# Spreading the DMA sums of w_down over the earlier stages of a hybrid pooling / RG-LRU / ConvFFN layer

## The chip, the cores and the metric

One core of one Trainium2 chip runs the whole layer as one program. The metric is the device time of one execution in microseconds (us). TensorE (PE) multiplies, VectorE (DVE) and ScalarE (ACT) do elementwise work, GpSimd (POOL) does a little arithmetic and issues DMAs, SyncE (SP) only issues DMAs.

## The reference, cut to what matters

One layer on 1024 tokens of width 1024 (a 16 x 64 grid) with 256 context tokens, all in float32:

```python
h = rmsnorm(x, g) * (1 + sc1) + sh1
u_pool, u_lru, u_gate, g_pool, g_lru = split(h @ w_in)
y_pool = grouped(pool(u_pool) - u_pool) @ pool_w * pool_scale
y_lru  = (scan_fwd(u_lru) + scan_bwd(u_lru)) * gelu(u_gate)
m = sigmoid(g_pool) * (y_pool @ w_proj_pool) + sigmoid(g_lru) * (y_lru @ w_proj_lru)
x = x + ga1 * rmsnorm(m @ w_out, g_post_mix)
g, u = split((rmsnorm(x, g_pre) * (1 + sc2) + sh2) @ w_up)     # 2 x 3072 columns
f = (gelu(conv3x3(g) + b) * u) @ w_down                        # 3072 -> 1024
out = x + ga2 * rmsnorm(f, g_post)
```

## The kernel before, in words

Every matrix product is done in three passes: both operands are split into a high float32r part (an ACT copy) and a low rest (a DVE subtraction), L89. The program goes through these stages, one after the other in time:

- **mixing** (to about 290 us): input norm, modulation, the pooling and gelu-gate units of w_in, pooling products. Stores: sg_d (L299), gl_d (L364), yp_d (L384).
- **LRU** (to about 570 us): for each of 8 channel blocks the input unit, four gate products, the scans, one sigmoid-gate unit. Stores: sg_d (L465), yl_d (L535). The square in the recurrence (L514) is POOL's.
- **projection** (to about 800 us): the remaining gate units with their sg_d stores (L575), the reloads of yp_d and yl_d (L566, L579), the two projections, whose result is stored to m_d (L604). Then the output projection (L706) and the first norm.
- **FFN up** (about 893 to 1400 us): 24 steps f. Each step makes one 128-channel pair of the gate and up halves by a seven-product block scheme, runs the 3 x 3 convolution on DVE (L900), the gelu on ACT (L912), the product on DVE (L913), and stores it to gu_d through POOL's queue (L917). For the seven products the weights of a step (two 512 KB loads from w_up, L681 and L796) are added together and split (L797 to L804).
- **FFN down** (to the end): the same scheme with seven products over 12 pairs p; it needs sums of blocks of w_down (sd_d) as well as w_down itself. finish (L1029) makes the last norm and the residual from x1_d and stores the output rows; half h = 1 is finished after product 5, half h = 0 after product 6, which is the last.

The sums sd_d are made by DMA alone, in the buffer n2raw. For each of the 12 pairs, sum_steps (L850) gives five steps: two plain loads, three accumulating DMAs, two accumulating DMAs, one accumulating DMA, two stores to sd_d. That is 10 DMAs for each pair, all issued from POOL's queue, and each step works on what the step before it left in n2raw, so it waits until that has landed. In the kernel before, the 60 steps are issued in the FFN up stage, three behind each step f from f = 0, so that they are done at f = 19:

```python
for _ in range(3):
    g = next(steps, None)
    if g is not None:
        with tc.issue_after(chain[-1].ins):
            chain.append(next(g)[-1])
```

n2raw also holds a term of the FFN input between the end of the projection stage (L674) and the start of the FFN (L764, L768), and a copy of u at f = 21 and 22 (L905).

The order on each engine is set by the planner's priorities, which follow the order of the program unless a line raises them; issue_after puts an instruction behind a given one on the same queue. An engine's queue is worked off in order: an instruction that waits holds up all that stand behind it. The w_up loads go through SP's queue into a ring of four buffers (tag raw, three of them, and rx): a load is issued when the DVE splits that read the buffer's old contents are done, and the ACT split (L89) of what it brings stands in ACT's queue ahead of the copy fk (L810), which frees a product's PSUM for the next.

Of the kernel before, what the change touches and what calls it, by code (L numbers as in the profile page):

```python
# [8 lines left out]
F32 = mybir.dt.float32  # L9
F32R = mybir.dt.float32r  # L10
AF = mybir.ActivationFunctionType
ALU = mybir.AluOpType
# [5 lines left out]
P = 128  # L18
# [22 lines left out]
def block_kernel(ctx: ExitStack, tc: tile.TileContext, x, cx, vecs, rowv, icnt, w_mod1, w_mod, w_in, pool_w,  # L41
                 lru_w, w_pp, w_pl, w_out, w_up, w_down, out):
    nc = tc.nc
    V, A, G, T = nc.vector, nc.scalar, nc.gpsimd, nc.tensor
# [18 lines left out]
    yl_d = tc.dram_tile([KT, P, SEQ], F32, name="yl_d")  # L63
    yp_d = tc.dram_tile([KT, P, SEQ], F32, name="yp_d")
    sg_d = tc.dram_tile([KT, P, 2, SEQ], F32, name="sg_d")
    gl_d = tc.dram_tile([KT, P, SEQ], F32, name="gl_d")
    m_d = tc.dram_tile([KT, P, SEQ], F32, name="m_d")
    x1_d = tc.dram_tile([SEQ, D], F32, name="x1_d")
# [12 lines left out]
    def uid(s):  # L81
        nm[0] += 1
        return f"{s}{nm[0]}"
# [14 lines left out]
        return w  # L98

    n2raw = gpool.tile([P, 4, 512], F32, name="n2raw", tag="n2raw")  # L100
    epsc = cpool.tile([P, 1], F32, name="epsc")
    G.memset(epsc, EPS)

# [183 lines left out]
    with tc.tile_pool(name="z1", bufs=1, reuse_waits="tile") as zp:  # L287
# [5 lines left out]
        def gate_unit(which, c):  # L293
            w = wload(24 + 8 * which + c)
            ps = pp.tile([P, SEQ], F32, name=uid("pg"), tag="pu")
            mm = unit_mm(ps, w, hx_act)
            s = zp.tile([P, SEQ], F32, name=uid("sg"), tag="sg", bufs=2)
            A.activation(s, ps, AF.Tanh, scale=0.5)
            G.dma_start(sg_d[c, :, which, :], s)  # L299
            return mm  # L300

        ds, pws, invs = {}, {}, {}
# [54 lines left out]
        def ug_unit(c):  # L357
            wu = wload(16 + c)
            pu = pp.tile([P, SEQ], F32, name=uid("pu"), tag="pu")
            n_unit[0] += 1  # L360
            mm = unit_mm(pu, wu, hx_act, half_outer=n_unit[0] <= NHO)
            gl = zp.tile([P, SEQ], F32, name=uid("gl"), tag="sg", bufs=2)
            A.activation(gl, pu, AF.Gelu_apprx_tanh)
            G.dma_start(gl_d[c], gl)  # L364
            return mm

        def pool_out(g, o, after):
            pw = pws[g]
            c = 2 * g + o
            yp = zp.tile([P, SEQ], F32, name=uid("yp"), tag="yp", bufs=2)  # L370
            for h in range(2):
                hs = slice(h * 512, (h + 1) * 512)
                ps = pp.tile([P, 512], F32, name=uid("pw"), tag="py", bufs=2)
                with tc.issue_after(after.ins):
                    for k in range(2):
                        for i, (wi, ai) in enumerate(((0, 0), (0, 1), (1, 0))):
                            T.matmul(ps, pw[:, wi, o, k, :], ds[2 * g + k][:, ai, hs],
                                     start=(k == 0 and i == 0), stop=(k == 1 and i == 2))
                with tc.high_priority(offset=YPRI):
                    if h == 0:  # L380
                        A.activation(yp[:, hs], ps, AF.Copy, scale=vcol("pool_scale", c))
                    else:
                        V.tensor_scalar(yp[:, hs], ps, vcol("pool_scale", c), None, op0=ALU.mult)
            G.dma_start(yp_d[c], yp)  # L384

        ctx_t = {}

# [66 lines left out]
    with tc.tile_pool(name="z2", bufs=1, reuse_waits="tile") as zp, \  # L454
# [3 lines left out]
        def gate_unit(which, c):  # L458
            w = load_w(w_in[24 + 8 * which + c])
            ps = pp.tile([P, SEQ], F32, name=uid("pg"), tag="pu", bufs=2)  # L460
            unit_mm(ps, w, hx_act)
            s = zp.tile([P, SEQ], F32, name=uid("sg"), tag="sg", bufs=2)
            with tc.high_priority(offset=SPRI):
                A.activation(s, ps, AF.Tanh, scale=0.5)
            G.dma_start(sg_d[c, :, which, :], s)  # L465

        LC = SEQ

# [19 lines left out]
        def lru_scan(c, xp, xc, wg):  # L488
# [43 lines left out]
            y = is_[0][:, 0:SEQ]  # L532
            V.tensor_add(y, y, is_[1][:, 0:SEQ])
            V.tensor_mul(y, y, gl)
            G.dma_start(yl_d[c], y)  # L535

        gq = [(0, c) for c in range(6)] + [(1, c) for c in range(KT)]
        mods = mod_steps(zp, pp, (2, 3), 2)
# [15 lines left out]
    with tc.tile_pool(name="pj", bufs=1, reuse_waits="tile") as zp:  # L554
# [14 lines left out]
        for j, (which, c) in enumerate(gq):  # L569
            w = load_w(w_in[24 + 8 * which + c])  # L570
            ps = pbank("bbcdbb"[j])
            unit_mm(ps, w, hx_act)
            s = zp.tile([P, SEQ], F32, name=uid("sg"), tag="mq", bufs=NMQ)
            A.activation(s, ps, AF.Tanh, scale=0.5)
            G.dma_start(sg_d[c, :, which, :], s)  # L575
        hy = H("hy")
        for c in range(KT):
            st = stage()
# [17 lines left out]
        def pl_unit(c):  # L596
            mp = mps.pop(c)
            s = sg_load(1, c)
            w = load_w(w_pl[c])
            ps = pbank("b")  # L600
            unit_mm(ps, w, lambda h, k, i: hy[:, h, k, i, :])
            V.scalar_tensor_tensor(s, s, 1.0, ps, op0=ALU.add, op1=ALU.mult)
            V.tensor_add(s, s, mp)
            G.dma_start(m_d[c], s)  # L604
            return s

        n_pc = [0]
# [43 lines left out]
            bcs.append(t)  # L651
        ga1g, B2, S2 = bcs

        h2 = H("h2")
        xos = []
        LATE = 5
# [96 lines left out]
    with tc.tile_pool(name="ff", bufs=1, reuse_waits="tile") as zp:  # L753
# [93 lines left out]
                V.tensor_sub(gc[:, 0, 512:1024], v, u4)  # L847
            st[f] = (gc, u2)

        def sum_steps(p):  # L850
            n2v = n2raw.rearrange("p (g h) c -> p g h c", g=2)
            lo, up = w_down[p * P:(p + 1) * P, :], w_down[(NH + p) * P:(NH + p + 1) * P, :]
            hv = lambda a: a.rearrange("p (h c) -> p h c", h=2)
            add = lambda dst, src: G.dma_start(dst, src, accum_op=ALU.add)  # L854
            yield G.dma_start(n2v[:, 0], hv(lo)), G.dma_start(n2v[:, 1], hv(up))
            yield (add(n2v[:, 1], hv(lo)), add(n2v[:, 0, 0, :], lo[:, 512:1024]),
                   add(n2v[:, 0, 1, :], lo[:, 0:512]))
            yield add(n2v[:, 1, 0, :], lo[:, 512:1024]), add(n2v[:, 0, 0, :], up[:, 512:1024])
            yield add(n2v[:, 1, 0, :], up[:, 512:1024]),
            yield tuple(G.dma_start(sd_d[p, i], n2v[:, i].rearrange("p h c -> p (h c)")) for i in range(2))  # L860

        steps = iter([st_ for p in range(NH) for st_ in [sum_steps(p)] * 5])
        chain = []

        def tail(f):
# [97 lines left out]
        for f in range(NF):  # L963
            if f + 1 < NF:
                weights(f + 1)
            mid(f)
            if f + 1 < NF:
                head(f + 1)
            tail(f)
            if f + 1 < NF:  # L970
                post(f)
            for _ in range(3):
                g = next(steps, None)
                if g is not None:
                    with tc.issue_after(chain[-1].ins):
                        chain.append(next(g)[-1])
        pre = [down_set(0, p, gpool.tile([P, D], F32, name=uid("raw"), tag="raw", bufs=3),
                        gpool.tile([P, 2, D], F32R, name=uid("whl"), tag="whl", bufs=3)) for p in range(NPRE)]

# [30 lines left out]
    with tc.tile_pool(name="dn", bufs=1, reuse_waits="tile") as zp:  # L1010
# [3 lines left out]
        def mms(q, p, op, t):  # L1014
            dst, first = PRODS[q][:2]
            for i, (gi, wi) in enumerate(((0, 0), (0, 1), (1, 0))):
                T.matmul(bank[dst](t), op[:, gi, 512 + t * P:512 + (t + 1) * P], op[:, wi, H0],  # L1017
                         start=(first and p == 0 and i == 0), stop=(p == NH - 1 and i == 2), skip_group_check=True)
# [7 lines left out]
        s0 = zp.tile([P, 16], F32, name="s0")  # L1026
        EPRI = 150

        def finish(h, t):  # L1029
            tt = 4 * h + t  # L1030
            xr = zp.tile([P, 2, 512], F32, name=uid("xr"), tag="xr", bufs=2)
            nc.sync.dma_start(xr, x1_d[tt * P:(tt + 1) * P, :].rearrange("p (h c) -> p h c", h=2))
            ss = small.tile([P, 1], F32, name=uid("ss"), tag="ss1", bufs=3)
            if h:
                y = CB[:, :, t, :]
                with tc.high_priority(offset=EPRI):
                    A.copy(CB[:, 0, t, :], bank["X"](t))
                A.activation(jk, y, AF.Square, accum_out=ss)
                V.tensor_mul(y, y, gah)
            else:  # L1040
                y = CA[:, :, t, :]
                V.tensor_sub(CA[:, 1, t, :], bank["Y"](t), CA[:, 1, t, :])  # L1042
                A.activation(jk[:, 1, :], CA[:, 1, t, :], AF.Square, accum_out=s0[:, 4 + t:5 + t])
                V.tensor_mul(CA[:, 1, t, :], CA[:, 1, t, :], gah[:, 1, :])
                V.tensor_add(ss, s0[:, t:t + 1], s0[:, 4 + t:5 + t])
            r = rstd_of(ss, 1)
            od = out[tt * P:(tt + 1) * P, :].rearrange("p (h c) -> p h c", h=2)
            for o in (slice(0, 1), slice(1, 2)) if tt == 3 else (slice(0, 2),):
                V.scalar_tensor_tensor(xr[:, o, :], y[:, o, :], r[:, 0:1], xr[:, o, :], op0=ALU.mult, op1=ALU.add)
                nc.sync.dma_start(od[:, o, :], xr[:, o, :])  # L1050

        GRP = 6
        for q in range(7):
            last = NH - GRP if q == 6 else NH
            for p in range(last):
                op = get(q, p)
                for t in range(4):
                    mms(q, p, op, t)
            if q == 6:
                ops = [get(q, p) for p in range(last, NH)]  # L1060
            for t in range(4):
# [97 lines left out]
```

## Time and profile before

| | |
|---|---|
| runs, median (lowest to highest) | 1640.2 us (1632.53 to 1645.49), 3 runs |
| the profiled execution | 1641.79 us, span 1640.0 us |
| PE busy | 1568.3 us, 96% of the span |
| DVE busy | 1210.5 us, 74% |
| ACT busy | 687.0 us, 42% |
| POOL busy | 239.3 us, 15% |
| mean granted clock of TensorE | 0.987 of full speed |
| moved by DMA | 289.15 MB |

The span runs from the first to the last instruction of the profiled execution; the time of an execution holds about 1.8 us more. [...]

### The profile page before, as it was taken

Reading aid. Unit: us, or ns where it says so; the run is one execution under the profiler, and the core shown is the slowest. Engines: PE = TensorE matmul, PEld = TensorE weight load, DVE = VectorE, ACT = ScalarE, POOL = GpSimd, SP = SyncE. Lnnn points to the kernel's source line nnn. Section 1 sums busy time; section 2 is a strip of 40 time slices with the busy share of each in tenths; the row PEclk is TensorE's granted clock in tenths of the full one; section 3 lists DMA queues with packets and bytes.
Section 4 is the critical chain, followed back from the end, with each engine's and each line's share of the span. In section 5 each row is a group of like instructions: output and inputs, shape, how many; then the busy total and the mean of one; then the engine's idle time right before and its main releaser. Section 6 shows DMA issues by size and latency. Waiting matters only on the chain.

```text
span 1640.0 us, 18320 instructions
## 1 busy us (share of the span) xinstructions
PE 1568.3 (96%) x6976; PEld 1265.2 (77%) x6976; DVE 1210.5 (74%) x1368; ACT 687.0 (42%) x828; POOL 239.3 (15%) x328
## 2 busy tenths in 40 slices
PE   6899999999999999999999989999899999999997
PEld 4588888877778788888788768877677777888885
DVE  7777664787887654354378889998798889787567
ACT  8523322565567734122143334333333334445442
POOL 1400200111112211010110122222222220000000
PEclk9999999999999999999999999999999999999999
DMA  8335454324233266399344567777667673687555
GB/s 314 114 103 165 138 184 139 127 97 148 84 103 116 90 232 230 124 289 300 131 141 142 209 195 186 193 199 197 176 183 180 178 187 110 217 320 256 175 188 192
DMA packets 98358, 289.15 MB, mean 176 GB/s; under 512 B 10871, under 2 KB 10999, under 8 KB 97502
## 3 DMA queue, kind: packets, MB, share of 16 engines
q1 hardware_dynamic: 60926, 170.64, 31.7%
q0 software_dynamic: 37344, 117.34, 24.2%
q8 instruction: 54, 0.88, 0.2%
q14 instruction: 34, 0.28, 0.1%
HBM read 221.34 MB, written 66.60 MB: 176 GB/s over the span
## 4 chain that ended last, share of the span: by engine, by line
PE 32%; DVE 10%; DMA 6%; ACT 2%; issue 2%; SPq 0%; DVEq 0%; ACTq 0%
PE pb L740 7%; PE pb L1017 6%; PE pb L706 5%; PE pc L740 4%; DMA raw<-in_w_up_dram 4%; PE pd L1017 4%; DVE gc L900 4%; PE pd L740 3%; PE pc L1017 2%; DVE wf L89 1%; DMA out_dram<-xr 1%; ACT wf L89 1%; DVE raw L801 0%; DMA xr<-x_d 0%; DVE w L89 0%
## 5 line engine op out<-in xcount | busy, mean ns | idle before, releaser
L242 PE MATMUL pu<-hx,whl 128*128 128x512 f32 x1056 | 266.7, 392 | 1.4 <-DVE whl L89 1.4
L900 DVE SCALAR_TENSOR_TENSOR gc<-gc,vec 128x945 f32<-128x945 f32 (+1 forms) x192 | 234.2, 1220 | 4.7 <-ACT gc L886 1.8
L89 ACT CAST whl<-raw 128x1024 fp32r<-128x1024 f32 (+1 forms) x109 | 109.1, 1003 | 305.8 <-DMA raw<-in_w_up_dram 74.4
L242 PEld LDWEIGHTS pu<-hx,whl 128*128 128x128 f32 x1056 | 186.8, 188 | 39.5 <-DVE whl L89 2.0
L89 DVE TENSOR_TENSOR whl<-raw,whl 128x1024 fp32r<-128x1024 f32 (+1 forms) x109 | 128.0, 1177 | 93.7 <-ACT whl L89 93.4
L242 PE MATMUL pg<-hx,whl 128*128 128x512 f32 x480 | 117.1, 396 | 0.0
L740 PE MATMUL pb<-h,wf 128*128 128x512 f32 x384 | 96.3, 400 | 11.3 <-ACT fk L810 11.3
L242 PEld LDWEIGHTS pg<-hx,whl 128*128 128x128 f32 x480 | 89.5, 191 | 19.3
L740 PEld LDWEIGHTS pb<-h,wf 128*128 128x128 f32 x384 | 71.8, 191 | 31.5 <-ACT fk L810 16.9
L740 PE MATMUL pb<-h,whl 128*128 128x512 f32 x384 | 94.9, 393 | 0.0
L706 PE MATMUL pb<-whl,mH 128*128 128x512 f32 x384 | 89.1, 392 | 1.0 <-ACT mH L700 1.0
L242 PE MATMUL pb<-hy,whl 128*128 128x512 f32 x384 | 87.8, 389 | 0.0
L706 PEld LDWEIGHTS pb<-whl,mH 128*128 128x128 f32 x384 | 71.5, 188 | 16.6 <-ACT mH L700 1.5
L740 PEld LDWEIGHTS pb<-h,whl 128*128 128x128 f32 x384 | 71.2, 188 | 16.9 <-ACT fk L810 2.5
L242 PEld LDWEIGHTS pb<-hy,whl 128*128 128x128 f32 x384 | 72.1, 188 | 14.9
L854 POOL DMA_DIRECT2D n2raw<-in_w_down_dram x72 | 63.0, 1006 | 122.9 <-DMA n2raw<-in_w_down_dram 122.6
L740 PE MATMUL pc<-nf,wf 128*128 128x512 f32 x288 | 72.9, 402 | 6.3 <-DVE gc L875 6.2
L1017 PE MATMUL pb<-hD 128*128 128x512 f32 x306 | 78.0, 390 | 0.0
L740 PEld LDWEIGHTS pc<-nf,wf 128*128 128x128 f32 x288 | 53.6, 190 | 22.5 <-DVE gc L875 11.5
L740 PE MATMUL pc<-nf,w 128*128 128x512 f32 x288 | 70.0, 391 | 0.2 <-DVE gc L847 0.2
L498 PE MATMUL pg<-xp,whl 128*128 128x512 f32 x192 | 61.3, 416 | 7.7 <-ACT i L504 7.6
L1017 PEld LDWEIGHTS pb<-hD 128*128 128x128 f32 x306 | 57.3, 188 | 12.3 <-DVE CA L1042 0.3
(319 smaller groups left out, 2986.9 us busy)
## 6 DMA issues: line engine op xcount, KB each, us to landing
raw<-in_w_up_dram SPq DMA_DIRECT2D x41, 512.0 KB, 4.6
raw<-in_w_in_dram SPq DMA_DIRECT2D x40, 512.0 KB, 4.7
n2raw<-in_w_down_dram POOLq DMA_DIRECT2D x36, 512.0 KB, 6.0
rawm<-in_w_mod_dram SPq DMA_DIRECT2D x32, 512.0 KB, 4.1
n2raw<-in_w_down_dram POOLq DMA_DIRECT2D x60, 256.0 KB, 5.7
rw<-gu_d SPq DMA_DIRECT2D x58, 256.0 KB, 5.1
gu_d<-gc POOLq DMA_DIRECT2D x24, 512.0 KB, 3.2
sd_d<-n2raw POOLq DMA_DIRECT2D x24, 512.0 KB, 4.6
```

Of the source, the lines that this page charges most:

```text
L89: return A.copy(hi, src), V.tensor_sub(lo, src, f32(hi))
L242: mm = T.matmul(ps[:, h * 512:(h + 1) * 512], wv[:, wi, k, :], act(h, k, ai), start=st, stop=sp)
L498: T.matmul(pg[:, h * 512:(h + 1) * 512], wg[:, wi, m, :], xp[:, ai, h * 512:(h + 1) * 512], start=(i == 0), stop=(i == 2))
L706: mm = T.matmul(ps[:, h * 512:(h + 1) * 512], mh[ai][:, k, :], wo[k][:, wi, h * 512:(h + 1) * 512], start=(k == 0 and i == 0), stop=(k == ...
L740: mm = T.matmul(ps, w(wi, j), b(ai, j), start=(start and j == 0 and i == 0), stop=(j == 3 and i == 2), skip_group_check=True)
L854: add = lambda dst, src: G.dma_start(dst, src, accum_op=ALU.add)
L900: V.scalar_tensor_tensor(o, gv[:, r0 + dr:r1 + dr, c0 + dc:c1 + dc], cw(i, j), o, op0=ALU.mult, op1=ALU.add)
L1017: T.matmul(bank[dst](t), op[:, gi, 512 + t * P:512 + (t + 1) * P], op[:, wi, H0], start=(first and p == 0 and i == 0), stop=(p == NH - 1 a ...
```

## The change

45 of the 60 steps are issued earlier: sum_step puts one step behind each store of the mixing, LRU and projection stages (there are 48 such stores; the first 45 get one, which makes pairs p = 0 to 8). The other 15 are issued in the FFN up stage, one behind each step f from f = 2 to f = 16. At the end of the program, the rows of x1_d that half h = 0 needs are loaded after product 5 into the first half of N, which no one reads any more then, in place of a buffer of two that the outputs also leave from.

```diff
+    def sum_steps(p):
+        ...
+    dsteps = [st_ for p in range(NH) for st_ in [sum_steps(p)] * 5]
+    n_step = [0]
+
+    def sum_step(after, limit=45):
+        if n_step[0] >= limit:
+            return after
+        with tc.issue_after(after.ins):
+            i = next(dsteps[n_step[0]])[-1]
+        n_step[0] += 1
+        return i
...
-            G.dma_start(sg_d[c, :, which, :], s)
+            sum_step(G.dma_start(sg_d[c, :, which, :], s))
...
-            G.dma_start(yl_d[c], y)
+            sum_step(G.dma_start(yl_d[c], y))
...
-            for _ in range(3):
-                g = next(steps, None)
-                if g is not None:
-                    with tc.issue_after(chain[-1].ins):
-                        chain.append(next(g)[-1])
+            if f > 1:
+                chain.append(sum_step(chain[-1], 60))
...
+        def load_x(xr, tt):
+            nc.sync.dma_start(xr, x1_d[tt * P:(tt + 1) * P, :].rearrange("p (h c) -> p h c", h=2))
+
         def finish(h, t):
             tt = 4 * h + t
-            xr = zp.tile([P, 2, 512], F32, name=uid("xr"), tag="xr", bufs=2)
-            nc.sync.dma_start(xr, x1_d[tt * P:(tt + 1) * P, :].rearrange("p (h c) -> p h c", h=2))
+            xr = N[:, 0, 2 * t:2 * t + 2, :] if h == 0 else zp.tile([P, 2, 512], F32, name=uid("xr"), tag="xr", bufs=2)
+            if h:
+                load_x(xr, tt)
...
+            if q == 5:
+                for t in range(4):
+                    load_x(N[:, 0, 2 * t:2 * t + 2, :], t)
```

The stores of gl_d, yp_d and m_d and the other two places that store sg_d are changed in the same way.

## Rows read from the trace of the kernel before

**Rows 1.** Windows of 100 us: busy us (instructions) by engine, granted clock, DMA share, GB/s.

```profile
700.00:800.00 100.00, 99.11 (x438) 81.79 (x436) 47.16 (x48) 22.59 (x26) 10.70 (x17) 1.00 0.81 263
...
900.00:1000.00 100.00, 89.45 (x372) 69.91 (x371) 86.47 (x96) 36.12 (x45) 18.55 (x29) 0.97 0.63 192
1000.00:1100.00 100.00, 99.80 (x434) 79.98 (x433) 94.87 (x99) 37.89 (x45) 25.67 (x36) 1.00 0.77 204
1100.00:1200.00 100.00, 93.44 (x393) 74.12 (x392) 83.69 (x88) 36.86 (x45) 23.22 (x33) 0.97 0.68 182
1200.00:1300.00 100.00, 92.56 (x394) 74.19 (x393) 87.88 (x90) 32.94 (x41) 21.77 (x31) 0.98 0.71 190
1300.00:1400.00 100.00, 96.89 (x419) 77.36 (x418) 88.45 (x91) 37.70 (x44) 17.01 (x24) 1.00 0.52 138
```

**Rows 2.** What PE waited for, whole run: total us, times, longest.

```profile
PE pb L740 <- ACT fk L810: 11.3, 8, 2.8
...
PE pg L498 <- ACT i L504: 7.6, 2, 3.8
```

**Rows 3.** Waits of the other engines, 880 to 1400 us.

```profile
ACT whl L89 <- DMA raw<-in_w_up_dram: 68.6, 18, 11.1
...
DVE gc L913 <- ACT gc L912: 13.2, 14, 1.2
```

**Rows 4.** The chain that ended last, 1140 to 1215 us: start, us, what.

```profile
1156.28 8.49 DMA raw<-in_w_up_dram
...
1167.37 5.23 PE pd L740 x12
```

**Rows 5.** POOL in order of time, 1148 to 1160 us: start, us, issues.

```profile
1149.36 1.06 POOL L855 DMA_DIRECT2D n2raw<-in_w_down_dram  x2
1154.65 2.64 POOL L854 DMA_DIRECT2D n2raw<-in_w_down_dram  x3 [4.23 <-DMA n2raw<-in_w_down_dram]
```

**Rows 6.** Loads of L681, 1000 to 1100 us.

```profile
DMA to landing us min/median/max: 4.3/4.7/5.0
```

**Rows 7.** Loads of L261 (512 KB of w_mod, mixing and LRU stages).

```profile
DMA to landing us min/median/max: 3.7/4.1/5.8
```

**Rows 8.** The same chain, whole run: first and last of twelve w_up loads.

```profile
951.14 7.03 DMA raw<-in_w_up_dram
...
1328.66 6.25 DMA raw<-in_w_up_dram
```

**Rows 9.** Windows of 20 us, columns as in the first group.

```profile
940.00:960.00 20.00, 13.80 (x52) 10.32 (x51) 16.33 (x18) 7.72 (x9) 4.29 (x6) 0.91 0.59 182
...
1160.00:1180.00 20.00, 14.80 (x55) 11.45 (x54) 11.78 (x13) 5.89 (x7) 2.84 (x4) 0.83 0.52 123
```

**Rows 10.** The end, in order of time.

```profile
1628.19 0.84 PE L1017 MATMUL pc<-hD 128*128 128x512 f32 x3
1629.96 1.28 DVE L1049 SCALAR_TENSOR_TENSOR xr<-CA,rs,xr 128x1024 f32<-128x1024 f32 x1 [2.34 <-DMA xr<-x_d]
1631.16 0.68 DVE L1042 TENSOR_TENSOR CA<-pc,CA 128x512 f32<-128x512 f32 x1
...
1635.55 1.42 DVE L1049 SCALAR_TENSOR_TENSOR xr<-CA,rs,xr 128x512 f32<-128x512 f32 x2 [0.94 <-DMA xr<-x_d]
```

**Rows 11.** The accumulating DMAs' line: duration ns of an issue, first and last start.

```profile
L854 POOL DMA_DIRECT2D n2raw<-in_w_down_dram x72: 848/873/1597, 956.0 to 1353.7; - x72
```

**Rows 12.** What POOL waited for, whole run.

```profile
POOL a L514 <- ACT r L512: 118.9, 15, 35.4
```

**Rows 13.** LRU stage about 380 us in order of time: POOL, SP's queue, ACT, PE.

```profile
377.67 0.56 POOL L535 DMA_DIRECT2D yl_d<-i  x1 [12.02 <-DVE i L534]
...
379.61 0.33 SPq L94 DMA_DIRECT2D raw<-in_w_in_dram  x1
...
385.90 1.04 ACT L89 CAST whl<-raw 128x1024 fp32r<-128x1024 f32 x1 [4.22 <-DMA raw<-in_w_in_dram]
...
388.02 1.22 PE L498 MATMUL pg<-xp,whl 128*128 128x512 f32 x2 [3.79 <-ACT i L504]
```

More of the change, by code (lines that the diff above doesn't have):

```diff
@@ L100, in block_kernel @@
     n2raw = gpool.tile([P, 4, 512], F32, name="n2raw", tag="n2raw")
+    def sum_steps(p):
+        n2v = n2raw.rearrange("p (g h) c -> p g h c", g=2)
+        lo, up = w_down[p * P:(p + 1) * P, :], w_down[(NH + p) * P:(NH + p + 1) * P, :]
+        hv = lambda a: a.rearrange("p (h c) -> p h c", h=2)
+        add = lambda dst, src: G.dma_start(dst, src, accum_op=ALU.add)
+        yield G.dma_start(n2v[:, 0], hv(lo)), G.dma_start(n2v[:, 1], hv(up))
+        yield (add(n2v[:, 1], hv(lo)), add(n2v[:, 0, 0, :], lo[:, 512:1024]),
+               add(n2v[:, 0, 1, :], lo[:, 0:512]))
+        yield add(n2v[:, 1, 0, :], lo[:, 512:1024]), add(n2v[:, 0, 0, :], up[:, 512:1024])
+        yield add(n2v[:, 1, 0, :], up[:, 512:1024]),
+        yield tuple(G.dma_start(sd_d[p, i], n2v[:, i].rearrange("p h c -> p (h c)")) for i in range(2))
+    dsteps = [st_ for p in range(NH) for st_ in [sum_steps(p)] * 5]
[7 more added lines that the diff above has]
+        return i
     epsc = cpool.tile([P, 1], F32, name="epsc")
@@ L363, in ug_unit @@
             A.activation(gl, pu, AF.Gelu_apprx_tanh)
-            G.dma_start(gl_d[c], gl)
+            sum_step(G.dma_start(gl_d[c], gl))
             return mm
@@ L383, in pool_out @@
                         V.tensor_scalar(yp[:, hs], ps, vcol("pool_scale", c), None, op0=ALU.mult)
-            G.dma_start(yp_d[c], yp)
+            sum_step(G.dma_start(yp_d[c], yp))
         ctx_t = {}
@@ L464, in gate_unit @@
                 A.activation(s, ps, AF.Tanh, scale=0.5)
-            G.dma_start(sg_d[c, :, which, :], s)
+            sum_step(G.dma_start(sg_d[c, :, which, :], s))
         LC = SEQ
@@ L574, in block_kernel @@
             A.activation(s, ps, AF.Tanh, scale=0.5)
-            G.dma_start(sg_d[c, :, which, :], s)
+            sum_step(G.dma_start(sg_d[c, :, which, :], s))
         hy = H("hy")
@@ L603, in pl_unit @@
             V.tensor_add(s, s, mp)
-            G.dma_start(m_d[c], s)
+            sum_step(G.dma_start(m_d[c], s))
             return s
@@ L652, in block_kernel @@
         ga1g, B2, S2 = bcs
+        assert n_step[0] == 45
         h2 = H("h2")
@@ L848, in mid @@
             st[f] = (gc, u2)
[L850 to L862, printed above, removed]
         chain = []
```

## The prediction, made before the changed kernel was run

> **What bounds the kernel now.** I read the busy time in windows first. PE works almost without a gap in every stage but one: even 700 to 800 us, the heaviest in DMA, keeps it busy 99.1 us of 100. The FFN up stage has the gaps [rows 1]. The count of instructions says more than the busy time, since a matmul at the lower clock is busy for longer: the stage's own best window did 434, the others 372, 393, 394 and 419. So 900 to 1000 us is 62 instructions short and 1100 to 1400 us 41 + 40 + 15 = 96. At 100 us / 434 = 0.23 us each these are 14.3 and 22.1 us. This 36 us is the most that the FFN can give back.
>
> Next the waits. PE's longest sum of waits is for the ACT copy fk, 11.3 us into the pb banks alone [rows 2]. A copy of half a bank isn't slow, so the question is what ACT did before it: ACT stood 68.6 us waiting for w_up loads, 11.1 us the longest time [rows 3]. The chain shows one case whole: a load issued at 1156.28 us lands 8.49 us later, ACT splits it and only then copies fk, and PE starts at 1167.37 us, where its twelve matmuls take 5.23 us for want of clock [rows 4]. At that moment POOL had just issued a step's two plain loads and three accumulating DMAs [rows 5]. So the step's traffic and the critical load were in flight together.
>
> How long is such a load otherwise? Where 1000 to 1100 us ran without gaps, L681's loads took 4.7 us in the middle, 4.3 the least [rows 6]. The same size in the mixing and LRU stages takes 4.1 us [rows 7]. On the chain stand twelve w_up loads between 951 and 1329 us [rows 8].
>
> **The change part by part.** The sum is made against the profiled execution, 1641.8 us (span 1640.0), which lies 1.6 us over the median of the runs.
>
> *FFN, 1100 to 1400 us: -17 us.* From f = 2 to 16 one step remains behind each gu_d store in place of three, and later none. The ten loads on the chain from 1103 us on average 5.65 us; at 4.1 us each is 1.55 us shorter, 15.5 us together. The other bound is the shortfall of 22.1 us, all of it gone: the half-speed matmuls behind a stall vanish with the stall, and the slice about 1160 us alone stood at 0.83 of the clock [rows 9]. I take 17 us, nearer to the loads' sum, since the remaining steps still meet a load now and then. What is late next is DVE: 94.87 us busy of 100 in the best window [rows 1]. If it binds, the gain is about 8 us; this is the low end.
>
> *FFN, start: -5 us.* The first steps come just before 950 us, and the load of 951.14 takes 7.03 us [rows 8]. In 940 to 980 us PE is slowed, with 52 instructions in the first half of it and a clock of 0.91 [rows 9]. The load falls to some 4.1 to 4.7 us (2.3 to 2.9 us), and the slow matmuls behind it win as much again. The gaps before that come from the norm's chain and stay. Bounds: 2 and 9 us.
>
> *The end: -3.0 us.* After PE's last matmul (1629.03 us) DVE is held by the residual of t = 2, which waits 2.34 us for its x rows; so L1042 of t = 3 starts at 1631.16 and not about 1629.1 us. At 1635.55 us t = 3 has waited 0.94 us for its own rows [rows 10]. With the rows there beforehand both go: 2.06 + 0.94 = 3.0 us. The four loads go out after product 5, into SP's queue ahead of the last product's loads; 2 MB beside a PE that has its operands ahead: nothing, or at worst 1 us.
>
> *The earlier stages: +4 us.* Nine pairs bring 90 DMA issues: 54 accumulating at 0.87 us [rows 11] and 36 plain at 0.53 us (a pair takes 1.06) [rows 5], 66 us of POOL over 45 stores, at most 2.6 us behind one store. POOL was busy 10.7 us of 100 at 700 us [rows 1] and mostly idle in the stages before, and what waits behind a step there is the next store, a memset, a reload of yp_d or yl_d or the square L514; but the square waits for ACT in 15 of its 16 times, 118.9 / 15 = 7.9 us on average [rows 12], so a step fits in ahead of it. A step that waits for the step before it (4.2 us at 1154 us [rows 5]) holds these up only where two stores lie closer than that, as the gate stores of the projection stage do; there PE works on the gates while the operands are reloaded. I cost POOL's queue at 1 us, bounds 0 and 4.
>
> The traffic costs more. In the LRU stage the yl_d store at 377.67 us and a w_in load at 379.61 us go out together; the load lands at 385.9, ACT has waited 4.22 us for it, and PE 3.79 us for ACT [rows 13]. The 22nd step, three accumulating DMAs of 1 MB, now goes out between them. The load then takes as long as it did now, or 4.4 us more (8.49 us against 4.1 [rows 4, 7]). I take 2 us there and 1 us for the other blocks, most of whose loads go out several us before or after the yl_d store. Bounds for all the earlier stages: -2 us (a shifted order can gain) and +8.
>
> [...]
>
> Sum: -17 - 5 - 3 + 4 = -21 us. 1641.8 - 21 = 1620.8 us, and from the median 1619.2; I say **1620 us**. The measurement of this kernel tells about 1% (16 us) from no change.
>
> **The rivals.**
>
> *DVE binds (1631 us).* With 94.87 us of DVE for 434 PE instructions [rows 1] a step f, 84 matmuls, costs 18.4 us of DVE in 19.4 us. On top DVE waits for the gelu, 13.2 us in 14 times [rows 3], 0.9 us each. That is 19.3 us: no slack at all. For it: 900 to 1400 us has DVE at 84 to 95 us of 100. Against it: the same best window shows PE at 99.8 us with three steps behind each f. Then the FFN gives 8 + 2, the end 3, the earlier stages take 4: -9 us.
>
> *The steps stay in the way (1640 us).* The planner sets each queue's order anew; if the shifted order of ACT and DVE in the FFN puts a load's split ahead of fk more often, the shorter loads are used up. Nothing in the profile speaks for it but that the order is the planner's; then the gain is the end's 3 us, less the earlier stages' 4.
>
> *All of it (1605 us).* 22 + 9 + 3 with the earlier stages at nothing: -34 us. The untroubled 1000 to 1100 us speaks for it.
>
> *Slower: the LRU loads pay (1660 us).* The 16 stores of the LRU stage each send a step's 0.25 to 1 MB beside the w_in, w_mod and lru_w loads, whose ACT splits stand ahead of the tanh that frees the gates' PSUM. PE has no slack where [rows 13] show it. A load that is 4.4 us longer holds PE for 4.4 us and the next matmuls lose about 1.5 us of clock. With eight of them, one for each block, this is 47 us, against the 25 us that the FFN and the end give: +22 us. It decides from 25 / 5.9, some four loads, on. Against it: only two waits, 7.6 us, for that ACT tanh in the whole stage [rows 2], and the loads of the other blocks lie away from the stores.
>
> **How the numbers follow.** Forecast 0.55, DVE binds 0.25, in the way 0.07, all of it 0.05, slower 0.08. Within the forecast the parts' bounds spread about 7 us to each side; 1% is 1623.8 us, so some three quarters of it is below, and with "all of it" and a little of the DVE case faster by over 1% has 0.50. Slower by over 1% is the last rival, 0.08. Same: 0.42. The range takes in the forecast's spread, the DVE case and nearly "all of it": 1606 to 1640 us.
>
> **What would show it.** Right: w_up loads on the chain at 4 to 4.7 us, ACT's wait for them down from 68.6 to under 40 us, and windows of 430 PE instructions or more in 1100 to 1400 us; accumulating DMAs from some 100 us on; at the end no wait for x rows, and L1042 of t = 3 within 0.3 us of PE's last matmul. DVE binds: short loads, but fk and L875 still late, DVE at 95 us of 100. Slower: PE waits on the tanh of L504 above 7.6 us, many of them with a w_in load over 6 us ahead. I'd be wrong if the FFN's shortfall stays though its loads are short, or if the projection stage, at 0.81 of the DMA engines' time [rows 1], loses PE time to the steps.

## The result, and the profile after

The changed kernel takes 1661.5 us (median of 4, 1661.1 to 1663.53) beside 1642.85 us for the kernel before: ratio 1.0127, 95% interval 1.0079 to 1.0175. It is 1.3% slower, where 1620 us was forecast. The profiled execution has a span of 1661.8 us and a mean granted clock of TensorE of 0.980 of full speed (0.987 before).

Where the time went is read by cutting the span at four matmuls: the first gate product of the LRU, the last one, the first product of the output projection, the first of the FFN; the last column runs from there to the end. All runs of this study stand in this table of profiled executions (us); the experiments are told below. Each row is a single execution. How far a row repeats is told by the kernel before, e1 and e4, which have no early step and the same order of PE, DVE and ACT up to the FFN: they differ by up to 0.8, 0.9, 1.8 and 0.1 us in the first four columns.

| kernel | mixing | LRU | projection | output projection | FFN up and down | span |
|---|---|---|---|---|---|---|
| before | 307.4 | 238.6 | 254.2 | 92.8 | 747.0 | 1640.0 |
| after | 321.5 | 250.4 | 274.9 | 94.3 | 720.7 | 1661.8 |
| e1 no early steps | 306.6 | 239.0 | 253.9 | 92.8 | 723.3 | 1615.6 |
| e2 bytes without waits | 320.2 | 241.3 | 264.2 | 92.8 | 722.9 | 1641.6 |
| e3 other places | 322.1 | 242.2 | 265.6 | 92.9 | 722.3 | 1645.1 |
| e4 end only | 307.0 | 239.5 | 255.7 | 92.9 | 747.9 | 1642.9 |
| e5 steps, old order | 324.4 | 256.9 | 273.6 | 94.2 | 721.8 | 1670.9 |
| e6 no steps, new order | 313.1 | 237.2 | 263.5 | 92.9 | 720.7 | 1627.5 |
| e7 bytes, old order | 320.4 | 243.9 | 265.3 | 92.9 | 722.5 | 1645.0 |
| e8 other places, old order | 324.0 | 237.6 | 257.0 | 94.3 | 722.1 | 1635.0 |
| e9 spread, old order | 308.2 | 238.3 | 267.2 | 95.2 | 729.0 | 1637.9 |
| e10 spread, free order | 308.7 | 242.1 | 268.7 | 95.4 | 729.2 | 1644.2 |
| e11 spread best | 308.4 | 239.3 | 258.4 | 95.2 | 728.1 | 1629.3 |
| e12 none in projection | 307.7 | 239.3 | 255.7 | 92.8 | 738.1 | 1633.6 |

So the FFN and the end gave back 747.0 - 720.7 = 26.3 us, as forecast (25). The three stages ahead lost 14.1 + 11.8 + 20.7 = 46.6 us, where 4 were forecast (and the output projection 1.5).

The windows of the kernel after, with the columns of [rows 1]:

```profile
300.00:400.00 100.00, 90.54 (x420) 72.85 (x420) 77.99 (x68) 55.69 (x55) 16.26 (x14) 0.97 0.45 143
400.00:500.00 100.00, 89.23 (x386) 72.01 (x387) 78.25 (x63) 61.21 (x59) 26.94 (x22) 0.90 0.48 142
...
900.00:1000.00 100.00, 94.83 (x429) 76.91 (x429) 85.48 (x129) 39.88 (x61) 8.84 (x16) 0.98 0.49 169
...
1100.00:1200.00 100.00, 98.95 (x431) 80.12 (x431) 93.67 (x98) 36.55 (x45) 10.20 (x15) 1.00 0.42 121
1200.00:1300.00 100.00, 99.27 (x432) 80.14 (x432) 95.36 (x99) 36.57 (x45) 10.20 (x15) 1.00 0.42 124
1300.00:1400.00 100.00, 98.16 (x426) 78.95 (x425) 93.45 (x97) 38.52 (x47) 3.77 (x7) 1.00 0.26 90
```

The FFN windows of 393, 394 and 419 instructions [rows 1] have become 431, 432 and 426. The gaps have moved to the LRU: 400 to 500 us does 386 instructions at a clock of 0.90. The kernel before did 446 there:

```profile
400.00:500.00 100.00, 95.59 (x446) 76.88 (x445) 84.92 (x70) 62.64 (x62) 19.78 (x13) 0.98 0.35 113
```

The waits of the whole run (columns of [rows 2]) say whom PE and POOL wait for now:

```profile
POOL n2raw L105 <- DMA n2raw<-in_w_down_dram: 57.7, 14, 8.9
...
PE pg L521 <- ACT i L527: 10.3, 3, 6.1
...
PE pb L265 <- ACT sg L487: 9.4, 1, 9.4
PE pd L265 <- DVE sgp L616: 5.9, 1, 5.9
PE pu L265 <- ACT whl L89: 4.8, 1, 4.8
PE pb L764 <- ACT fk L834: 4.4, 7, 0.8
```

The last row answers to the 11.3 us of [rows 2]. The first is POOL's queue standing still: a step waits for the step before it, 14 times, up to 8.9 us. Such waits are not new. The kernel before had more of them, in the FFN:

```profile
POOL n2raw L854 <- DMA n2raw<-in_w_down_dram: 122.6, 39, 7.5
```

So such a wait is not dear by itself (e8 below has the same steps in the LRU at 237.6 us, beside 238.6 in the kernel before); what counts is what stands behind it on the queue.

What that does in the LRU, in order of time (POOL, SP's queue, ACT and PE; line numbers in this stage are 23 higher than before, the square is L537):

```profile
391.31 0.53 POOL L558 DMA_DIRECT2D yl_d<-i  x1 [10.75 <-DVE i L557]
391.84 1.07 POOL L106 DMA_DIRECT2D n2raw<-in_w_down_dram  x2
...
393.21 0.33 SPq L94 DMA_DIRECT2D raw<-in_w_in_dram  x1
...
401.10 1.04 ACT L89 CAST whl<-raw 128x1024 fp32r<-128x1024 f32 x1 [6.27 <-DMA raw<-in_w_in_dram]
401.15 2.74 POOL L105 DMA_DIRECT2D n2raw<-in_w_down_dram  x3 [8.25 <-DMA n2raw<-in_w_down_dram]
...
403.21 1.22 PE L521 MATMUL pg<-xp,whl 128*128 128x512 f32 x2 [6.08 <-ACT i L527]
...
405.01 3.55 POOL L537 TENSOR_TENSOR a<-r 128x1280 f32<-128x1280 f32 x1 [1.12 <-ACT r L535]
```

One block shows both mechanisms. Two steps stand behind the yl_d store, not one: in the program the yl_d store comes ahead of the same block's sg_d store, but on POOL's queue sg_d goes out first, and its step, which is the later one by number, has to wait behind yl_d's. The second step waits 8.25 us for the first, with the next block's square behind it on the queue. That time the square was held little; in five other blocks it starts right behind such a step, with no wait of its own, for instance here:

```profile
363.45 0.55 POOL L111 DMA_DIRECT2D sd_d<-n2raw  x1 [5.00 <-DMA n2raw<-in_w_down_dram]
364.01 2.34 POOL L537 TENSOR_TENSOR a<-r 128x1280 f32<-128x1280 f32 x1
```

And the w_in load issued at 393.21 us lands only at 401.1, 7.9 us, with the step's two loads in flight (in [rows 13] such a load took 6.3 us). Over the whole run DVE waits 41.8 us for the square, up to 6.9 us at a time, where it was 28.9 us and up to 3.7 before.

In the projection POOL's queue is one row of such waits. The steps there hold the reloads L589 and L602 and the gate stores L598:

```profile
628.12 0.85 POOL L105 DMA_DIRECT2D n2raw<-in_w_down_dram  x1 [8.89 <-DMA n2raw<-in_w_down_dram]
...
668.80 1.74 POOL L105 DMA_DIRECT2D n2raw<-in_w_down_dram  x2 [5.42 <-DMA n2raw<-in_w_down_dram]
...
683.47 0.53 POOL L111 DMA_DIRECT2D sd_d<-n2raw  x1 [6.49 <-DMA n2raw<-in_w_down_dram]
```

The chain that ended last (columns of [rows 4]) runs straight through them:

```profile
661.07 7.45 DMA n2raw<-in_w_down_dram
...
669.36 6.79 DMA n2raw<-in_w_down_dram
...
683.99 4.86 DMA st<-yl_d
...
693.75 4.00 DMA st<-yl_d
...
697.77 1.05 ACT hy L89
...
699.99 1.23 DVE sgp L616
...
701.35 10.77 PE pd L265 x40
```

Two steps, then the reloads that stood behind them; DVE splits the last reload ahead of L616, which frees the PSUM that PE waits for.

In mixing the chain runs through two loads that grew. Three stores between 273 and 284 us had each sent a step, the last one's three accumulating DMAs at 288.37 us:

```profile
289.94 10.42 DMA rawm<-in_w_mod_dram
...
301.76 6.01 DMA raw<-in_w_in_dram
```

The w_mod loads took 4.1 us in the middle before and 5.8 us at most [rows 7]; that longest one was this same load, which now takes 10.42 us. The end came out as forecast, to be read against [rows 10]:

```profile
1652.88 0.84 PE L1025 MATMUL pc<-hD 128*128 128x512 f32 x3
1653.76 0.69 DVE L1054 TENSOR_TENSOR CA<-pc,CA 128x512 f32<-128x512 f32 x1
...
1657.26 1.41 DVE L1061 SCALAR_TENSOR_TENSOR N<-CA,rs,N 128x512 f32<-128x512 f32 x2
```

No wait for x rows is left. From the last matmul's start to the last residual are 4.38 us, 7.36 before.

### The profile page after: what moved, and what is told of

Same layout as the page of the kernel before. It is cut to its first block, busy times and chain, and to the rows that moved or that the text cites. A ratio compares the mean times of both kernels' runs of the same rounds, so it can differ in the third digit from the quotient of the medians.

```text
span 1661.8 us, 18309 instructions
## 1 busy us (share of the span) xinstructions
PE 1574.9 (95%) x6976; PEld 1270.9 (76%) x6976; DVE 1217.7 (73%) x1368; ACT 684.8 (41%) x828; POOL 240.2 (14%) x328
## 4 chain that ended last, share of the span: by engine, by line
PE 63%; DMA 11%; DVE 10%; issue 8%; ACT 4%; POOL 3%; SPq 0%; DVEq 0%; POOLq 0%; ACTq 0%
PE pb L764 11%; PE pu L265 9%; PE pc L764 7%; PE pb L1025 7%; PE pb L730 5%; PE pd L764 5%; PE pd L1025 4%; PE pc L1025 3%; PE pg L265 2%; DMA raw<-in_w_in_dram 2%; PE pb L265 2%; DMA n2raw<-in_w_down_dram 2%; DMA rawm<-in_w_mod_dram 2%; PE pd L265 1%; PE pg L521 1%
## 5 line engine op out<-in xcount | busy, mean ns | idle before, releaser
L265 PEld LDWEIGHTS pu<-hx,whl 128*128 128x128 f32 x1056 | 191.1, 191 | 47.5 <-ACT whl L89 5.2
L928 POOL DMA_DIRECT2D gu_d<-gc x24 | 13.1, 547 | 430.8 <-DVE gc L924 430.8
L105 POOL DMA_DIRECT2D n2raw<-in_w_down_dram x72 | 64.3, 1080 | 59.6 <-DMA n2raw<-in_w_down_dram 57.7
L289 DVE SCALAR_TENSOR_TENSOR acc<-rawm,cs,acc 128x1024 f32<-128x1024 f32 x28 | 39.4, 1406 | 43.4 <-DMA rawm<-in_w_mod_dram 43.4
```

The costliest lines, as they stand in the source:

```text
L265: mm = T.matmul(ps[:, h * 512:(h + 1) * 512], wv[:, wi, k, :], act(h, k, ai), start=st, stop=sp)
L289: V.scalar_tensor_tensor(acc, raw, cs[:, k, 0:1], acc, op0=ALU.mult, op1=ALU.add)
L928: chain.append(G.dma_start(gu_d[f], gc[:, 1, :]))
```

## The experiments

Three theories stood at first: POOL's queue (a step that waits holds the square, the reloads and the stores behind it), traffic (the stages' loads land later beside the steps' bytes), and the planner (it gives the engines another order).

**e1, no early steps.** The FFN's 15 steps and the preload stay.

```diff
+        if n_step[0] < 45:
+            n_step[0] += 1
+            return after
```

The down stage then reads w_down's rows in place of the nine pairs' sums that are not formed.

> The changed kernel without its 45 early steps: the 15 steps behind the FFN's blocks and the preloaded x rows stay, the sums of the first nine pairs are not formed and their w_down rows are read raw in their place, so the output differs. In the changed kernel's profile the LRU's first gate matmul stands at 321.4 us (before: 307.3), the LRU's gate matmuls span 250.5 us (before 238.7), and from there to the output projection's first matmul are 274.9 us (before 254.1). If the early steps cost those 47 us, by POOL's queue or by traffic, the three go back to about 307, 239 and 254, and the time is about 1661 - 47 = 1615 us (1610 to 1622). If the cost is in the new order of the engines' work and not in the steps, some of the three stay as long as in the changed kernel and the time stays above 1640.

Measured: 1617.2 us, ratio 0.9846 (0.9805 to 0.9887). All three stages are back. The 45 steps cost what was missing, and the FFN's gain is whole without them. It doesn't judge the planner, since without the early steps PE, DVE and ACT have the kernel before's order again up to the FFN.

**e2, the bytes without the waits.**

```diff
+        if n_step[0] < 45:
+            p, k = divmod(n_step[0], 5)
+            with tc.issue_after(after.ins):
+                for j, n in enumerate(((1024, 1024), (1024, 512, 512), (512, 512), (512,), (1024, 1024))[k]):
+                    i = G.dma_start(cp_d[p, 3 * k + j, :, 0:n], w_down[(p + NH * (j % 2)) * P:(p + NH * (j % 2) + 1) * P, 0:n])
```

> The changed kernel with each of the 45 early steps replaced by transfers of the same number and bytes at the same places, which copy w_down's rows to a place in DRAM that nothing reads: no accumulation and no wait for the step before (the sums of the first nine pairs are left out, the output differs). Queue theory (a step that waits on POOL's queue for the step before it holds the square, the reloads and the gate stores behind it): the three stages go most of the way back, to about 310, 240 and 256 us, and the time is 1617 to 1628 us. Traffic theory (the loads of the stages land later beside the steps' bytes): the stages stay at about 320, 249 and 272 us and the time at 1652 to 1662 us.

Measured: 1642.4 us, ratio 1.0002 (0.9978 to 1.0026): between the two. Mixing keeps its loss (320.2), the LRU loses most of it (241.3), the projection half (264.2). Neither theory alone holds.

**e3, the same steps in other places.**

```diff
# LRU: both steps of a block behind its gate store
-            sum_step(G.dma_start(sg_d[c, :, which, :], s))
+            sum_step(sum_step(G.dma_start(sg_d[c, :, which, :], s)))
...
-            sum_step(G.dma_start(yl_d[c], y))
+            G.dma_start(yl_d[c], y)
...
# projection: behind the last reload of yl_d
+        for _ in range(6):
+            last_ld = sum_step(last_ld)
```

> The changed kernel with the same 60 steps in other places: in the LRU both steps of a block stand behind its gate store and none behind its yl store, so that on POOL's queue no step stands right ahead of the next block's square; the projection stage's six steps stand behind the last reload of yl instead of behind the gate stores. Same bytes, same sums. Queue theory: mixing stays at about 321 us, the LRU goes from 250.5 to about 241 and the stretch to the output projection from 274.9 to about 256, the time is about 1661 - 9 - 19 = 1633 us (1627 to 1642). Traffic theory: within 6 us of the changed kernel, 1655 to 1662.

Measured: 1646.8 us, ratio 1.0034 (1.0013 to 1.0056). The LRU is at 242.2 as the queue theory had it, but the projection at 265.6 and not at 256.

**e4, the end only.** The preload in the kernel before.

> The kernel before with the preloaded last x rows alone; every step stays where it was. The last store's chain behind PE's last matmul was 1635.55 - 1628.19 us with the add of x 1.77 us behind the multiply. If the load's lateness alone cost that, the span is 3 us shorter (1637 us beside 1640, within the noise of one run, so read in the profile: from PE's last matmul to the last store's start 4.4 us or so instead of 7.4) and the stages ahead are as in the kernel before.

Measured: one execution, 1644.7 us. From PE's last matmul (1634.05 us) to the last residual (1638.42) are 4.37 us. The 3 us are the preload's; the total of one run can't show it.

In e2 and e3 PE has one gap of 9.35 us at the projection's start, whatever the steps do, and the kernel after has it too (9.4 us in the waits above). That pointed at the order. Compared instruction by instruction, up to the FFN the planner has put 175 of 3928 matmuls, 49 of 676 DVE and 27 of 403 ACT instructions elsewhere than before; in e2 and e3 every matmul stands as in the kernel after. So the next runs hold the order of PE, DVE and ACT up to the FFN: an edge on the same engine from each instruction to the next one, in a listed order. POOL's and SP's queues are left to the planner.

```diff
+    pin_order(tc, nc)
...
+        for a, b in zip(order, order[1:]):
+            tc.add_manual_dep(row[b], row[a].name, mybir.DependencyInfo(
+                mybir.DependencyClass.NoSync, mybir.DependencyReason.DATA), reason="pin")
```

**e5, the kernel after in the old order.**

> The changed kernel with all 60 steps where they are, but with the instructions of PE, DVE and ACT up to the FFN held in the kernel before's own order (the planner, which models the steps' bytes, had put 175 of 3928 matmuls, 49 of 676 DVE and 27 of 403 ACT instructions in other places). Up to the FFN the changed kernel loses 14.1 us in mixing, 11.8 in the LRU and 20.7 in the stretch to the output projection. If the steps themselves cost that (queue and traffic), the three stay near 321, 250 and 275 us and the time at 1655 to 1662. If the new order costs what the same bytes without waits still cost (12.8, 2.7 and 10.0 us), it falls by some 20 us, to about 1640.

Measured: 1668.7 us, ratio 1.0173 (1.0142 to 1.0204), above both expectations. With the steps running, the old order is worse, by 2.9 us in mixing and 6.5 in the LRU.

**e6, the new order without the early steps.**

> The kernel without the 45 early steps (1617 us), with PE, DVE and ACT up to the FFN held in the changed kernel's order: the order alone, without a step's bytes or waits (the sums of the first nine pairs are not formed, the output differs). If the order costs nothing by itself, 1617 us with the stages at 307, 239 and 254 us. If the order is what the copies without waits paid for, 1635 to 1642 us with mixing at about 320 and the projection stretch at 264.

Measured: 1629.6 us, ratio 0.9932 (0.9908 to 0.9957), 12.5 us over e1: 6.5 in mixing, 9.6 in the projection, -1.8 in the LRU. ACT and PE at the projection's start, in order of time:

```profile
559.15 1.28 ACT L530 ACT_TABLE_LOAD   x1 [6.45 <-DVE i L548]
...
570.35 1.02 ACT L490 ACTIVATE sg<-pg 128x1024 f32<-128x1024 f32 x1
...
571.42 23.92 PE L268 MATMUL pb<-hx,whl 128*128 128x512 f32 x96 [9.37 <-ACT sg L490]
```

ACT waits 6.45 us for DVE, works off the last block's gates and exponents, and only then copies the finished gate unit out of PSUM, for which PE waits 9.37 us. In the old order (e5) the gap at that point is 1.35 us.

**e7, bytes without waits in the old order.**

> The run with the steps' bytes as copies without waits, with PE, DVE and ACT up to the FFN held in the kernel before's order: the bytes alone (sums of the first nine pairs left out, the output differs). If bytes delay the stages' loads by themselves: about 1642 us as with the new order, stages 320, 241 and 264. If the new order made that cost: about 1617 to 1622 us, stages 307 to 310, 239 to 241 and 254 to 257.

Measured: one execution, 1646.8 us; the stages are at 320.4, 243.9 and 265.3. The bytes cost by themselves. The gap in the projection has gone to another place; PE in order of time:

```profile
577.73 22.06 PE L274 MATMUL pb<-hx,whl 128*128 128x512 f32 x96 [1.77 <-ACT i L536]
673.33 13.46 PE L274 MATMUL pc<-yps,whl 128*128 128x512 f32 x48 [8.26 <-DVE sgp L625]
```

The projection's products now wait for what the late reloads and gate stores hold up: on e7's chain two reloads of yl_d take 12.31 and 9.82 us, though POOL waits at most 1.03 us right ahead of either.

**e8, e3's places in the old order.**

> The 60 steps with the LRU's steps all behind gate stores and the projection stage's behind the last reload of yl, with PE, DVE and ACT up to the FFN held in the kernel before's order. If the queue's places cost about 15 to 18 us and the order about 25, both are gone here and little is left: 1617 to 1625 us, faster than the kernel before. If bytes cost 25 us by themselves: about 1643 us.

Measured: 1637.9 us, ratio 0.9974 (0.9957 to 0.9991). The LRU (237.6) is free of loss with 16 steps in it, the projection (257.0) nearly so with 11. What is left is mixing, at 324.0. So in these two stages the same steps with the same bytes cost next to nothing at these places in the old order, while the new order (e6) and the bytes at the first places (e7) each cost something alone. The time is above the first expectation by what mixing still loses.

**e9, fewer steps in mixing.** Mixing keeps the steps behind its stores 1 to 3 and 9 to 12. n2raw is taken by other data while a pair is half formed (by the FFN's input after step 38, and at f = 21 and 22), so the sums of two pairs come out different, in e10 too.

```diff
+    def mix_step(after):
+        n_at[0] += 1
+        return sum_step(after) if n_at[0] in MIX else after
```

> All 60 steps, other places: 7 in mixing (behind its first three stores and its ninth to twelfth, none between 130 and 195 us or after 250), 16 in the LRU behind gate stores, 10 behind the last reload of yl, 5 behind m_d stores, 22 behind the FFN's blocks; PE, DVE and ACT up to the FFN held in the kernel before's order. Against the reordered run with that order (stages 324.0, 237.6, 257.0 us, 1637.9 us in all) only mixing should change much: if its 17 us come from the bytes landing beside the loads at 135 to 175 and 252 to 300 us, mixing is at 307 to 312 and the time at 1622 to 1630 us with some 3 us of the FFN's gain given back. If any steps in mixing cost as much, it stays at 320 or more and the time at 1638.

Measured: 1641.6 us, ratio 0.999 (0.9976 to 1.0004), against the expected 1622 to 1630. Mixing is at 308.2, as expected. But with ten steps behind the last reload the projection takes 267.2 us, and seven more steps in the FFN, the last of them behind f = 23, cost 7 us in the last column. In the projection ACT waits 27.4 us for w_out loads, up to 9.0 us at a time (12.7 us in the kernel before), and PE for ACT. PE in order of time:

```profile
772.82 7.36 PE L271 MATMUL pb<-hy,whl 128*128 128x512 f32 x20 [5.91 <-ACT whl L89]
...
813.69 26.63 PE L738 MATMUL pb<-whl,mH 128*128 128x512 f32 x104 [4.59 <-ACT mH L732]
```

**e10, the same with the order left free.**

> The same places of the steps, with the engines' order left to the planner (13 of 403 ACT and 10 of 676 DVE instructions up to the FFN stand elsewhere than in the kernel before, no matmul). If the order is worth nothing beside the places, within 3 us of the same kernel with the order held; if these few moves matter as the full set did (13 us in the run of the new order without steps), up to 10 us slower.

Measured: 1642.0 us, ratio 0.9986 (0.9968 to 1.0004): no difference from e9 in the medians.

**e11, the best places found.** MIX = 1, 2, 3, 8 to 12; six steps behind the last reload; two behind each of the FFN's blocks f = 2 to 9, then one; order held.

> All 60 steps: 8 in mixing (none between 130 and 170 us or after 235), 16 in the LRU behind gate stores, 6 behind the last reload of yl, 5 behind m_d stores, 25 behind the FFN's blocks (two behind each of the first eight, so that none is later than before block 19); PE, DVE and ACT up to the FFN held in the kernel before's order. If the stages' costs add up as the runs so far gave them (mixing 308, LRU 238, projection stretch 257, output projection 94, the FFN some 4 us more than with 15 steps: 464, down 261), the time is 1622 to 1626 us, 1.0 % under the kernel before's 1641. If taking the steps out of one stage only moves the wait to the next, as in the run with ten steps behind the last reload (267 us there), 1635 or more.

Measured: 1629.8 us (6 runs), ratio 0.9905 (0.9878 to 0.9931), faster than both kernels, though above the expected 1622 to 1626. Some 14 us over e1 in the spans: 4.5 in the projection, 2.4 in the output projection, 4.8 in the FFN, 1.8 in mixing. The windows from 300 us on show PE's work back:

```profile
300.00:400.00 100.00, 95.16 (x442) 76.79 (x441) 77.87 (x69) 63.09 (x64) 20.98 (x18) 0.97 0.46 139
400.00:500.00 100.00, 95.15 (x445) 76.78 (x444) 86.22 (x71) 62.22 (x61) 27.39 (x25) 0.98 0.55 159
500.00:600.00 100.00, 98.17 (x441) 79.84 (x440) 65.52 (x51) 57.86 (x56) 28.62 (x27) 0.98 0.54 160
600.00:700.00 100.00, 100.00 (x443) 82.77 (x442) 45.72 (x43) 33.95 (x36) 22.94 (x38) 1.00 0.78 250
```

The DMA engines carry as much in 400 to 600 us as in the kernel after or more (share 0.55 beside 0.48 at 400), yet 445 instructions are done instead of 386.

**e12, no step in the projection.** Nine in mixing, two behind each of the first thirteen FFN blocks. The last pair is formed while n2raw holds u, so its sums differ.

> The same with no step in the projection stage: 9 in mixing, 16 in the LRU behind gate stores, 35 behind the FFN's blocks (two behind each of the first thirteen); order held as before up to the FFN. The projection stretch should be back at 254 and the output projection at 93 us (4 us less than with eleven steps there); the FFN pays for ten more steps: by 32 us for the 45 more that the kernel before has there (494.6 against 461), 7 us, to about 469. Together 1622 to 1630 us. If the FFN's cost comes only from three steps in one block and not from two, it stays at 462 and the time at 1616 to 1620.

Measured: 1641.1 us, ratio 0.998 (0.9964 to 0.9996), above both expectations; the profiled execution, at 1635.4, is the fastest of twelve and some 6 us under the median. The projection and the output projection are back at 255.7 and 92.8; the FFN up and down take 10.0 us more than in e11, more than expected: two steps behind a block cost too, and where steps go on to f = 23, here as in e9, the down stage is longer (266.4 and 266.6 us beside 261.5 in e11). Why the medians lie higher stays open.

## Why the prediction was wrong

**Right: the FFN.** Forecast -17 - 5 = -22 us; measured 26.3 less the end's 3.0, so -23.3. By its signs: windows of 430 instructions were named, and two of three are there. The w_up loads, median of the whole run, fell from 4.6 to 3.6 us, further than the 4.1 taken, and on the chain that ended last three of them are left, of 3.4 to 4.2 us, where twelve stood [rows 8]. ACT's wait for them fell from 68.6 us [rows 3] only to 52.9 (47.5 when the window is moved by the 48 us that the stage starts later), not under 40, though fk's own wait (11.3 to 4.4 us) did what counts: much of ACT's wait had never held PE. DVE at 93 to 95 us of 100 beside a PE at 98 to 99 took nothing back, so the DVE rival falls. One thing stays open: the planner reordered the FFN too (at least 184 of 3040 matmuls from its first product on stand elsewhere than before), the same way in the kernel after and in e1 to e3 and e5 to e8, and no run holds that order, so how much of the 23.3 us is the lighter traffic's and how much the order's is not shown.

**Right: the end.** -3.0 us forecast, 7.36 - 4.38 = 2.98 measured, and shown alone by e4.

**Wrong: "The earlier stages: +4 us".** Measured +46.6. The failed step is this term, and the sign that the prediction had named for it came: the projection stage loses PE time to the steps. It failed in three places:

1. *"So a step fits in ahead of it"*, POOL's queue at 1 us. The 7.9 us average was compared with the time of issuing a step (at most 2.6 us), and it holds one wait of 35.4 us [rows 12]; the other 14 average 6.0 us. What stands ahead of the square is a step that waits for the step before it to land, 4.4 to 8.3 us in the LRU, and two of them bunch behind one store because the queue's order isn't the program's. In the kernel after the waits cost 250.4 - 241.3 = 9.1 us in the LRU and 10.7 in the projection (after against e2, same matmul order); in the old order 13.0 and 8.3 (e5 against e7). e3 and e8 show it without a change in what a step does: with the 16 steps off the yl_d store the LRU takes 8.2 us less in the new order and 19.3 us less in the old one, where nothing of its loss is left. The copies of e2 and e7 are not quite the steps' traffic: they are plain and go to DRAM (one on e7's chain takes 13.23 us), so these differences also hold what an accumulation into n2raw costs the DMA engines more or less than that; in e8 the accumulations cost the LRU nothing behind the gate stores, but at the yl_d store the two are not separated.
2. *"There PE works on the gates while the operands are reloaded."* The gates end at 661 us, and the reloads were pushed past that: the last one of yl_d is issued at 693.75 us and lies on the chain, 32 us behind the gates' end (15 us in the kernel before, 640.29 against 624.87).
3. *"1 us for the other blocks."* Mixing was not priced by itself. It has 18 of the 48 stores and loses 14.1 us, of which copies without waits keep 12.8. PE's gaps there are at 174 us (4.20 us) and 304 us (4.84 us). The first is for the context rows (xs), for whose two loads ACT waits 13.1 us in place of 8.2; the second is for the split of the w_in load issued at 290.48 us, right behind the w_mod load of 10.42 us. Without steps about these points (e9, e11) mixing is at 308. That w_mod load took 10.42 us beside the steps against 5.8 for the same load before, and mixing is where that decides.

On the first point, this case's trace shows a queue worked off in order: POOL did nothing else in the 57.7 us of these waits, and right behind the longest, of 8.89 us, two reloads of yp_d went out at 628.68 us with no wait of their own.

**What the order adds.** The prediction priced a loss by the planner's order in the FFN alone; for the stages ahead it allowed only a gain, of 2 us. In front of it the new order costs 12.5 us without steps (e6 against e1). Yet it isn't to be added to the rest: with the steps running the same order gains 7 us (after against e5). By one path (e1, e6, e2, after) the 47 us are order 14, bytes 12, waits 21; by the other (e1, e7, e5, after) bytes 30, waits 25, order -8. How much is the order's is therefore not one number; that bytes and waits both cost is common to the two. (e7 is a single execution.)

**The slower rival** was given 0.08 and 1660 us. Its sign and time came out, its mechanism only for a part: eight LRU loads at 5.9 us were to make 47 us there, and the LRU lost 11.8. (The 1.5 us of clock in each 5.9 were the author's estimate; in the kernel before the twelve matmuls at 1167.37 us, behind a wait of 5.20 us, took 5.23 us, and the twelve at 1172.90 us 2.90.) So 1660 us came close by luck: mixing and the projection, which it left out, made up the rest. (Its own sum, +22 us from the median, is 1662, and that of "all of it", -34 us, is 1606, not 1605.) The range (to 1640) had no room for it, because the bounds of the failed term (-2 to +8) were drawn about issue times and one load, and none about a stage whose POOL queue stands still.

## What to carry to other kernels

An operation that is put behind a store in an in-order queue must be priced by the longest wait it can bring there (the landing of what it depends on, here up to 8.9 us), for everything that is queued behind it, and in the queue's order, not the program's. Moved traffic needs a price for each stage it enters, from the loads of that stage that have no slack now. Where a planner orders the engines by modelled times, hold the order fixed to tell the change from the reordering, and expect the two not to add.

## What was not expected of the hardware

A w_mod load of 512 KB took 10.42 us with a step's three accumulating DMAs just ahead of it (5.8 us for the same load before). In the LRU POOL stood 8.25 us for a step's landing and a w_in load took 7.9 us, in windows of 100 us whose DMA share was 0.45 and 0.48. Yet e8 keeps PE busy all the time at a share of 0.97:

```profile
700.00:800.00 100.00, 100.00 (x443) 82.81 (x442) 50.58 (x56) 25.71 (x31) 20.09 (x30) 1.00 0.97 318
```

So in these runs the mean share says little about what one transfer meets, or what a stage loses by it.

The clock made a gap dearer. With the 9.36 us gap that ends at 593 us the window from 580 to 600 us of the kernel after had PE at 0.74 of the clock and 35 instructions, where the next 20 us do 90 at 1.00. By an estimate from these rows the gap takes the place of some 42 of them; the rest took 10.64 us for 35, where 48 would have fitted at the full clock:

```profile
580.00:600.00 20.00, 10.64 (x35) 8.21 (x34) 9.40 (x8) 12.75 (x12) 9.02 (x9) 0.74 0.54 144
```
